# A feed-forward pass over two row groups at a time: one unit of gate or up weights for both groups of a half

## The chip, the cores and the metric

The kernel runs on one core of a Trainium2 chip. The metric is the time of one execution on the device in microseconds. Work is spread over five engines, each with its own in-order queue of instructions: TensorE (PE in the profile, with PEld for its weight loads) multiplies matrices into PSUM banks, VectorE (DVE) and ScalarE (ACT) move results out of PSUM and do elementwise work, GpSimd (POOL) does elementwise work between buffers in SBUF, and SyncE (SP) issues the transfers between SBUF and HBM.

## The reference

One layer of a hybrid encoder on 2048 rows of width 1024. The attention part (stick-breaking heads, chunked heads and a short convolution, normed per head to `y`) is the same in both kernels. What matters here is the part behind it:

```python
x = x + y @ w_out[l]                                          # output projection, 1024 x 1024
x = x + swiglu(rmsnorm(x, ffn_norm_w[l]), w_gate[l], w_up[l], w_down[l])

def swiglu(x, w_gate, w_up, w_down):                          # 1024 x 2816, 1024 x 2816, 2816 x 1024
    return (jax.nn.silu(x @ w_gate) * (x @ w_up)) @ w_down
```

The kernel holds every operand of these products as a high and a low part, and each product of a tile is three matmuls (high by high, high by low, low by high).

## The kernel before, in words

The 2048 rows are four groups of 512, numbered 0 to 3, in two halves: `HALVES` is [[3, 2], [1, 0]]. The first part of the program (`weave`, up to about 1168 us) runs the projections and the attention of both halves, then the output projection (`out_proj`) of groups 3 and 2, and makes group 3 ready for the feed-forward part (`operands`). `out_proj` writes x + y @ w_out to the HBM buffer `x1d`.

The feed-forward part is the function `ffn` (L1312). Its width of 2816 is cut into 22 tiles of 128 and `NP` = 11 pairs `p` of them. A *unit* (g, p, i) is the gate (i = 0) or up (i = 1) product of group g with pair p. It is done as seven products instead of eight (`Unit`, a1 to a5, b1, b2: Strassen's scheme in Winograd's form, two by two blocks), each of twelve matmuls of 128x256 in fp16 (`product`, L1165). The order is `units`: all 22 units of group 3, then 22 each of groups 2, 1 and 0, that is 88 units.

- **Weights of a unit.** Seven blocks, each high and low, lie in the tiles `wa` (4 blocks, 1 MB) and `wb` (3 blocks, 0.75 MB), two buffers each. For group 3 they are *made*: `unit_load` fetches two raw tiles, `unit_norm` sums squares on ScalarE (L959), `unit_scale` turns this into a power of two by a small matmul (L967) and five tiny VectorE operations, `unit_make` scales the raw tiles on ScalarE (L988), forms sums and differences on VectorE (L997, tiles `S`), casts the high parts on ScalarE (L992) and subtracts the low parts on GpSimd (L993), and stores the result to HBM (`u`). Groups 2, 1 and 0 fetch it from there (`unit_fetch`, L1017). A unit's weights are made or fetched in the turn two units ahead of it.
- **Down product.** When both units of a pair are done, `b2` splits silu(gate) * up into `gh` and `gl` (L1245, L1246, two buffers each), and `down` multiplies them by the two tiles of `w_down` (`load_down`: raw tile `wr`, then `wh` on ScalarE and `wl` on VectorE, L310, L312) and adds to the rows `x1` (L1271). It is called for half of the group's rows (24 matmuls of 128x512) in each of the next two units, so `w_down` is loaded and split once for each group and pair, 44 times two tiles. The raw tiles of gate, up and `w_down` share one ring `wr` of four buffers.
- **Side work** is put between the products of a unit by generators, a few steps at a time (`run_side`): in group 3 the per-head norms of the second half's y (`y_side`, L837 to L844, eight row tiles) and then the operands of group 2; in groups 2 and 1 the output projection of the next group (`proj_side`, one PSUM bank `av`) and then its operands. Whatever is left is run ahead of the next group (`run_all`). `operands` fetches x1, norms it (L367 to L372), turns it by 32 transposes (L908), forms seven blocks (L920) and splits them (L915, L916).

The order on TensorE is the order of the program text (`manual_schedule`). The other queues, SP's among them, are ordered when the program is built, by a planner that walks through the program with costs of its own: it takes the earliest instruction of the text whose inputs and buffers are free, so a transfer can be issued well before its place in the text, and the order it finds is fixed from then on.

Of the kernel before, what the change touches and what calls it, by code (L numbers as in the profile page):

```python
# [40 lines left out]
def trunk(ctx: ExitStack, tc: tile.TileContext, x, anw, w_in, qnw, knw, biasx, conv_w, onw, w_out,  # L41
# [466 lines left out]
    def proj_N(H, groups, units, use, prep=None):  # L508

        for g in groups:  # L510
            hh, hl = H.get(g, (None, None))
            for t in range(0, 4, 2):
                if prep is not None:
                    yield from prep.need(g, t)
                    hh, hl = H[g]
                o, bk = acc() if stream.paced else bank("av", 1)
                steps = chain.from_iterable(
                    mm3(o[:, s * 256:(s + 1) * 256], lambda k, cs=cs: hh[:, k, cs],
                        lambda k, cs=cs: hl[:, k, cs], lambda k: units[k // 4][0][:, k % 4],
                        lambda k: units[k // 4][1][:, k % 4], KT, 0.33)  # L520
                    for s, cs in ((s, slice((t + s) * 128, (t + s + 1) * 128)) for s in range(2)))
                yield from prep.beside(steps) if prep is not None else steps
                behind(bk.read(lambda g=g, t=t, o=o: use(g, t, o)))
# [354 lines left out]
    def operands(g, tmp, turn):  # L878
# [18 lines left out]
        for t in range(2):  # L897
# [20 lines left out]
            def less(a, b):  # L918
                f = tmp()
                nc.vector.tensor_tensor(f, a, b, ALU.subtract)  # L920
                return f
# [6 lines left out]
            t1 = less(b12, b11)  # L928
# [4 lines left out]
            t3 = less(b22, b12)  # L933
            parts(4, t3)
            t2 = less(b22, t1)
# [4 lines left out]
            parts(5, less(b21, t2))  # L940
# [41 lines left out]
    def unit_make(p, i):  # L982
# [12 lines left out]
        def made(op, a, b):  # L995
            f = fp.tile([128, 512], F32, name="S", tag="S", bufs=4)
            nc.vector.tensor_tensor(f, a, b, op)  # L997
            return f
# [9 lines left out]
        parts(wb[:, 2], made(ALU.subtract, a12, s2))  # L1008
# [73 lines left out]
    stream = Weights(HALF * 2 + OUT * NG)  # L1082
# [79 lines left out]
    order = [g for groups in HALVES for g in groups]  # L1162
    units = [(g, p, i) for g in order for p in range(NP) for i in range(2)]
# [16 lines left out]
    class Unit:  # L1180
# [7 lines left out]
        def got(self, f, t, c):  # L1188
            g, p, i = self.key
            ds = UD[p, i][1]  # L1190
            if i == 0:
                if (g, p) not in SG:
# [13 lines left out]
        def a1(self):  # L1206
            o = self.mul(0, acc)
            self.s1 = q("s1", 2)
            nc.scalar.copy(self.s1, o)
# [18 lines left out]

        def c_of(self, o, u, f, t):
            c = q("c", 2)  # L1230
            nc.vector.tensor_tensor(c, o, u, ALU.add)  # L1231
            self.got(f, t, c)
# [19 lines left out]
    def x1_load(g):  # L1252
        X1[g] = []
        for t in range(4):
            x1 = fp.tile([128, D], F32, name="x1", tag="x1", bufs=4)
            nc.sync.dma_start(x1, x1d[g * 4 + t])
            X1[g].append(x1)

    def down(g, p, ts):
        for t in ts:  # L1260
            cs = slice(t * 128, (t + 1) * 128)
            for c in range(2):
# [3 lines left out]
                for j, ((gh, gl), (wh, wl)) in enumerate(zip(G[g, p], DW[g, p])):  # L1266
# [6 lines left out]
    def s_tile():  # L1273
        return fp.tile([128, 512], F32, name="S", tag="S", bufs=4)

    def y_side():

        gain = gain_row("o")
        for g in HALVES[1]:
            for t in range(4):  # L1280
# [4 lines left out]
                y_norm(T, yt, gain, lambda: fp.tile([128, 512], F32, name="ysq", tag="S", bufs=4))  # L1285
                yield

    def proj_side(g):
        H = {}
        yield from out_proj(H, [g], stream, y_rows(H, [g]))  # L1290

    def operands_side(g):
        yield from operands(g, s_tile, tpb)

    second = HALVES[1]
    sides = {}
    for n, g in enumerate(order):
        steps = []
        if n == 0:
            steps.append(y_side())  # L1300
        if n + 1 < len(order):
            nxt = order[n + 1]
            if nxt in second:
                steps.append(proj_side(nxt))
            steps.append(operands_side(nxt))
        sides[g] = chain.from_iterable(steps)

    def run_side(g, n):
        for _ in islice(sides[g], n):
            pass  # L1310

    def ffn():  # L1312
        run = {}
        norms = {}
        made = {}
        made[units[0]] = unit_make(0, 0)
        made[units[1]] = unit_make(0, 1)
        for n in (2, 3):
            if n < len(units):
                unit_load(*units[n][1:])  # L1320
        x1_load(order[0])
        last = None
        n1 = 2 * NP
        for n, u in enumerate(units):
            g, p, i = u
            new = n < n1 - 2
            if new and units[n + 2] not in norms:
                norms[n + 2] = unit_norm(*units[n + 2][1:])
            if g not in BS:
                run_all(sides[units[n - 1][0]])  # L1330
            U = Unit(g, p, i, made.pop(u))
# [5 lines left out]
            per = 3 if n >= n1 else 2  # L1337
            run_side(g, per)
            U.a3()
            run_side(g, per)  # L1340
            U.a4()
            if new:
                unit_scale(*units[n + 2][1:], norms.pop(n + 2))
            if n + 2 < len(units):
                nu = units[n + 2]
                made[nu] = unit_make(*nu[1:]) if new else unit_fetch(*nu[1:])
            prev = (g, p - 1) if p else (order[order.index(g) - 1], NP - 1)
            if prev in G:
                down(*prev, (0, 1) if i == 0 else (2, 3))
            if i == 1:  # L1350
                if prev in G:
                    del G[prev], DW[prev]
                    if p == 0:
                        for t in range(4):
                            T = prev[0] * 4 + t
                            nc.sync.dma_start(out[T * 128:(T + 1) * 128, :], X1[prev[0]][t])
                        x1_load(g)
                DW[g, p] = [load_down(f) for f in (2 * p, 2 * p + 1)]
            if n + 4 < n1:
                unit_load(*units[n + 4][1:])  # L1360
            U.a5()
            run_side(g, per)
# [3 lines left out]
        g = order[-1]  # L1366
        down(g, NP - 1, range(4))
        for t in range(4):
            T = g * 4 + t
            nc.sync.dma_start(out[T * 128:(T + 1) * 128, :], X1[g][t])  # L1370

    with tc.manual_schedule(engines={mybir.EngineType.PE}):
        ffn()
# [33 lines left out]
```

## Time and profile before

| | us |
|---|---|
| median of 3 runs (range) | 2829.3 (2827.76 to 2829.47) |
| the profiled execution's own time | 2829.39 |
| its span, first to last instruction | 2827.6 |
| TensorE busy in the span | 2491.9 (88%) |
| VectorE, ScalarE, GpSimd busy | 1886.5, 1249.7, 591.3 |

The span is what the trace covers; 1.8 us of the execution lie outside it. Busy time of TensorE counts matmuls from issue to their modelled end, so it is an upper bound on useful work. The granted clock is the share of full speed that TensorE was given.

### The profile page before, as it was taken

The page shows a single profiled execution, that of the slowest core. Times are in us where ns is not written, and L with a number is a line of the kernel's source. Part 1 is how long each engine was busy: PE and PEld are TensorE (multiplying, and loading weights), DVE is VectorE, ACT ScalarE, POOL GpSimd, SP SyncE. Part 2 cuts the span into 40 slices and gives each one's busy share as a digit, 9 for nine tenths or more (in the row PEclk, how much of TensorE's full clock was granted, in tenths as well). Part 3 has the DMA queues.
Part 4 walks back from the last instruction along what each step waited for, and adds up shares of the span by engine and source line. Part 5 has one row for each costly group of instructions (what it writes and reads, how often), then busy time and mean ns, then how long its engine had stood idle before and what let it go on. Part 6 is the DMA issues. An engine that isn't in the chain of part 4 may idle for free. (4 is left out here: it accounts for less than half of the span.)

```text
span 2827.6 us, 50313 instructions
## 1 busy us (share of the span) xinstructions
PE 2491.9 (88%) x19448; PEld 2017.8 (71%) x19448; DVE 1886.5 (67%) x4181; ACT 1249.7 (44%) x2380; POOL 591.3 (21%) x635
## 2 busy tenths in 40 slices
PE   6998888997899888665878799997999997999999
PEld 4477767566776776544666688876788886888887
DVE  6478767699989868697766665444654446555555
ACT  5566656664566867655545431112321113221121
POOL 2234331103321223454644410000200002000000
PEclk9999999998899999877898899999999998999999
DMA  7443344523311565665544555454455444465442
GB/s 237 129 134 110 108 144 127 159 65 130 109 62 55 173 180 163 202 226 171 186 153 160 171 198 188 163 164 160 164 196 173 157 154 134 144 223 167 161 164 79
DMA packets 264688, 434.33 MB, mean 154 GB/s; under 512 B 79616, under 2 KB 196352, under 8 KB 253184
## 3 DMA queue, kind: packets, MB, share of 16 engines
q1 hardware_dynamic: 264448, 431.12, 47.2%
q8 instruction: 152, 2.49, 0.4%
q14 instruction: 88, 0.72, 0.1%
HBM read 321.46 MB, written 109.58 MB: 152 GB/s over the span
## 5 line engine op out<-in xcount | busy, mean ns | idle before, releaser
L1271 DVE TENSOR_TENSOR x<-tp,x 128x512 f32<-128x512 f32 x352 | 242.5, 690 | 212.7 <-PE tp L1269 212.5
L1267 PE MATMUL tp<-wh,gh 128*128 128x512 f32 x704 | 296.4, 421 | 61.7 <-ACT wh L310 24.2
L378 PE MATMUL acc<-w,hh 128*128 128x256 f16 x1152 | 325.1, 282 | 3.8 <-ACT w L273 3.8
L379 PE MATMUL acc<-w,hh 128*128 128x256 f16 x1152 | 324.7, 282 | 1.8 <-POOL w L274 1.8
L380 PE MATMUL acc<-w,hl 128*128 128x256 f16 x1152 | 324.2, 281 | 0.0
L1268 PE MATMUL tp<-wl,gh 128*128 128x512 f32 x704 | 286.8, 407 | 13.6 <-DVE wl L312 13.5
L1269 PE MATMUL tp<-wh,gl 128*128 128x512 f32 x704 | 285.0, 405 | 1.1 <-DVE gl L1246 1.1
L1196 ACT ACTIVATE sg<-c,ud 128x256 f32<-128x256 f32 x176 | 89.3, 508 | 424.3 <-DVE c L1231 406.9
L668 DVE SCALAR_TENSOR_TENSOR wtl<-tp,wth 128x512 f16<-128x512 f32 (+3 forms) x384 | 198.7, 533 | 51.5 <-ACT wth L663 50.6
L1231 DVE TENSOR_TENSOR c<-sc,u 128x256 f32<-128x256 f32 x264 | 111.1, 422 | 182.6 <-PE sc L1172 181.7
L733 DVE TENSOR_TENSOR_SCAN re<-re,zero 128x512 f32<-128x512 f32 (+3 forms) x160 | 191.4, 1196 | 39.8 <-ACT re L730 39.4
L310 ACT CAST wh<-wr 128x1024 fp32r<-128x1024 f32 x88 | 88.7, 1043 | 289.5 <-PE tp L1268 243.0
L663 ACT ACTIVATE wth<-tp 128x512 f16<-128x512 f32 (+3 forms) x384 | 173.5, 477 | 83.4 <-PE tp L659 82.1
L1267 PEld LDWEIGHTS tp<-wh,gh 128*128 128x128 f32 x704 | 138.4, 197 | 97.9 <-ACT wh L310 27.1
L1171 PE MATMUL sc<-bx,wb 128*128 128x256 f16 x704 | 192.3, 273 | 0.0
L1170 PE MATMUL sc<-bx,wb 128*128 128x256 f16 x704 | 192.3, 273 | 0.0
L1172 PE MATMUL sc<-bx,wb 128*128 128x256 f16 x704 | 192.3, 273 | 0.0
L379 PEld LDWEIGHTS <-hh 128*128 128x128 f16 x1408 | 141.7, 101 | 46.9 <-issue 20.4
L1171 PEld LDWEIGHTS <-wa 128*128 128x128 f16 x1408 | 140.0, 99 | 44.1 <-issue 26.0
L1268 PEld LDWEIGHTS tp<-wl,gh 128*128 128x128 f32 x704 | 138.6, 197 | 44.2 <-DVE wl L312 18.1
L916 POOL TENSOR_TENSOR hh<-S,hh 128x512 f16<-128x512 f32 x12 | 15.6, 1302 | 712.7 <-ACT hh L915 712.7
L1269 PEld LDWEIGHTS tp<-wh,gl 128*128 128x128 f32 x704 | 138.5, 197 | 35.9 <-DVE gl L1246 5.0
(246 smaller groups left out, 7121.6 us busy)
## 6 DMA issues: line engine op xcount, KB each, us to landing
wa<-u SPq DMA_DIRECT2D x66, 1024.0 KB, 4.9
wb<-u SPq DMA_DIRECT2D x66, 768.0 KB, 4.4
wr<-in_w_down SPq DMA_DIRECT2D x88, 512.0 KB, 4.1
w<-wd SPq DMA_DIRECT2D x48, 512.0 KB, 4.2
u<-wa SPq DMA_DIRECT2D x22, 1024.0 KB, 4.7
u<-wb SPq DMA_DIRECT2D x22, 768.0 KB, 4.4
wd<-w SPq DMA_DIRECT2D x32, 512.0 KB, 3.0
q<-qd SPq DMA_DIRECT2D x192, 64.0 KB, 2.3
```

What stands on the lines that cost most here:

```text
L378: nc.tensor.matmul(o, sh(k), mh(k), start=(k == 0), stop=False)
L379: nc.tensor.matmul(o, sh(k), ml(k), start=False, stop=False)
L380: nc.tensor.matmul(o, sl(k), mh(k), start=False, stop=(k == n - 1))
L668: nc.vector.scalar_tensor_tensor(wl[:, s], tp[:, :(b1 - b0) * 128], WSC, wh[:, s], op0=ALU.mult, op1=ALU.subtract)
L733: nc.vector.tensor_tensor_scan(re, re, zero.to_broadcast([128, N]), 1.0 if b == T else e[:, 0:1], ALU.mult, ALU.add)
L1170: nc.tensor.matmul(o, ah, bh, start=k == 0, stop=False)
L1171: nc.tensor.matmul(o, ah, bl, start=False, stop=False)
L1172: nc.tensor.matmul(o, al, bh, start=False, stop=k == 3)
L1267: nc.tensor.matmul(o, gh[:, cs], wh[:, cc], start=j == 0, stop=False)
L1268: nc.tensor.matmul(o, gh[:, cs], wl[:, cc], start=False, stop=False)
L1269: nc.tensor.matmul(o, gl[:, cs], wh[:, cc], start=False, stop=j == 1)
L1271: nc.vector.tensor_tensor(x1, o, x1, ALU.add)
```

## The change

The feed-forward part runs once per half, and the two groups of the half take turns with the same weights: after the first pair, (first, p, 0), (other, p, 0), (first, p, 1), (other, p, 1). In the first pair both units of the first group come before those of the other, while the other's operands are made. So gate and up weights are made in the first half (22 units) and fetched once in the second (22 units instead of 66 fetches), and `w_down` is loaded once per half and pair (22 times two tiles instead of 44). A unit's weights are made or fetched in the first group's turn with the unit before it; the turns a and b of one unit are the same instructions as before. `down` comes behind b2 and ahead of a2, and works off a list, one entry of two row tiles per turn. The rows `x1` of both groups are held (those of odd groups in the four tiles `w16`). The output projection of groups 1 and 0, and the operands of group 1, run between the two passes (`between`), with two PSUM banks (`acc`) instead of one.

To make room, `sg` has four buffers and `S`, `s1` and `c` have one less each; sums are written in place; three of seven splits in `operands` go from GpSimd to VectorE.

```diff
@@ proj_N
-                o, bk = acc() if stream.paced else bank("av", 1)
+                o, bk = acc()
@@ operands
-                nc.gpsimd.tensor_tensor(B[o][:, 1, :, cs], fv, B[o][:, 0, :, cs], ALU.subtract)
+                (nc.vector if o % 2 else nc.gpsimd).tensor_tensor(B[o][:, 1, :, cs], fv, B[o][:, 0, :, cs],
+                                                                  ALU.subtract)
...
-            t1 = less(b12, b11)
+            t1 = less(b12, b11, b11)
...
@@ class Unit, c_of
-                SG[g, p] = [fp.tile([128, 512], F32, name="sg", tag="sg", bufs=2) for _ in range(2)]
+                SG[g, p] = [fp.tile([128, 512], F32, name="sg", tag="sg", bufs=4) for _ in range(2)]
...
-                nc.scalar.activation(sg, c, AF.Silu, scale=ds)
+                nc.vector.tensor_tensor(sg, o, u, ALU.add)
+                nc.scalar.activation(sg, sg, AF.Silu, scale=ds)
...
@@ x1_load
+            if g % 2 == 0:
+                x1 = fp.tile([128, D], F32, name="x1", tag="x1", bufs=4)
+            else:
+                x1 = f32(wp.tile([128, 2, D], F16, name="w16", tag="w16").rearrange("p j c -> p (j c)"))
...
@@ ffn
+    def ffn(half, sides, tail):
+        first, other = HALVES[half]
+        weights = [(p, i) for p in range(NP) for i in range(2)]
+        turns = [(g, 0, i) for g in (first, other) for i in range(2)]
+        turns += [(g, p, i) for p in range(1, NP) for i in range(2) for g in (first, other)]
+        new = half == 0
...
+        begin(0)
+        DW[0] = [load_down(f) for f in (0, 1)]
+        begin(1)
+        for w in range(2, 4 if new else 0):
+            unit_load(*weights[w])
+        for g in HALVES[half]:
+            x1_load(g)
...
+            if g == other and p == 0 and i == 0:
+                run_all(sides)
+            U = Unit(g, p, i, made[p, i])
             U.a1()
             if last is not None:
                 last.b1()
                 last.b2()
+                lg, lp, li = last.key
+                if li == 1:
+                    due += [(lg, lp, (0, 1)), (lg, lp, (2, 3))]
+            if todo is not None:
+                tg, tp, ts = todo
+                down(tg, tp, ts)
+                if ts[0] == 2:
+                    del G[tg, tp]
+                    if tg == other:
+                        del DW[tp]
+                        if tp + 1 < NP:
+                            DW[tp + 1] = [load_down(f) for f in (2 * tp + 2, 2 * tp + 3)]
+            if (g == first and p > 0) or (g == other and (p, i) == (0, 1)):
+                if w + 1 in norms:
+                    unit_scale(*weights[w + 1], norms.pop(w + 1))
+                begin(w + 1)
+            if new and g == other:
+                if 4 <= w + 3 < len(weights):
+                    unit_load(*weights[w + 3])
+                if w + 2 < len(weights):
+                    norms[w + 2] = unit_norm(*weights[w + 2])
             U.a2()
+            side(3)
             U.a3()
+            side(3)
             U.a4()
+            side(3)
             U.a5()
...
+        for tg, tp, ts in due:
+            down(tg, tp, ts)
+            if (tg, ts[0]) == (first, 2):
+                store(first)
+            if tg == other:
+                for _ in islice(tail, 4):
+                    pass
+        store(other)
+        run_all(rest)
+        run_all(tail)
+
+    def between():
...
+        yield from out_proj(H, [a], W, rows)
+        yield from beside_of(out_proj(H, [b], W, rows), operands(a, s_tile, tpb))
...
+        ffn(0, (operands(HALVES[0][1], s_tile, tpb), y_side()), between())
+        ffn(1, (operands(HALVES[1][1], s_tile, tpb), iter(())), iter(()))
```

`begin(n)` makes (first half) or fetches (second half) the weights of unit n once; `side(n)` runs n steps of the other group's operands in the first group's first two turns, and of `y_side` after them.

## Rows read from the trace of the kernel before

**Rows 1.** Busy time by engine (page): us, share of the span, instructions.

```profile
PE 2491.9 (88%) x19448; PEld 2017.8 (71%) x19448; DVE 1886.5 (67%) x4181; ACT 1249.7 (44%) x2380; POOL 591.3 (21%) x635
```

**Rows 2.** Windows: length, busy PE, PEld, DVE, ACT, POOL, clock, DMA, GB/s.

```profile
1171.50:1669.80 498.30, 361.61 (x2376) 290.94 (x2377) 351.58 (x668) 260.09 (x430) 248.77 (x176) 0.85 0.55 185
1669.80:2078.50 408.70, 380.02 (x2827) 324.06 (x2826) 213.30 (x386) 86.38 (x148) 19.70 (x14) 0.97 0.51 170
2078.50:2482.20 403.70, 378.56 (x2826) 323.78 (x2824) 212.18 (x385) 86.51 (x148) 18.81 (x14) 0.98 0.47 159
2482.20:2827.60 345.40, 338.93 (x2450) 288.85 (x2448) 191.12 (x349) 66.17 (x112) 0.00 (x0) 1.00 0.47 158
1373.40:1637.80 264.40, 217.77 (x1432) 176.86 (x1430) 171.79 (x311) 141.08 (x231) 122.62 (x91) 0.90 0.51 166
2500.00:2800.00 300.00, 300.00 (x2213) 256.96 (x2211) 165.98 (x306) 60.13 (x102) 0.00 (x0) 1.00 0.48 161
```

**Rows 3.** Timeline of PE, first matmuls of units: start us, us, instruction.

```profile
1892.71 0.27 PE L1170 MATMUL acc<-hh,wa 128*128 128x256 f16 x1
1910.34 0.27 PE L1170 MATMUL acc<-hh,wa 128*128 128x256 f16 x1
...
2702.53 0.27 PE L1170 MATMUL acc<-hh,wa 128*128 128x256 f16 x1
2702.64 0.27 PE L1171 MATMUL acc<-hh,wa 128*128 128x256 f16 x1
...
2717.22 0.27 PE L1170 MATMUL acc<-hh,wa 128*128 128x256 f16 x1
```

**Rows 4.** Waits of PE, 1373 to 1638 us: total us, times, longest.

```profile
PE tp L1267 <- ACT wh L310: 17.8, 6, 3.3
PE sc L1170 <- DVE u L1227: 12.7, 5, 3.3
PE tp L1267 <- ACT gh L1245: 11.0, 6, 2.9
PE tp L1268 <- DVE wl L312: 4.1, 6, 1.8
PE tp L1269 <- DVE gl L1246: 1.1, 6, 0.2
```

**Rows 5.** Waits of all engines, 1373 to 1638 us.

```profile
DVE S L997 <- ACT wr L988: 15.4, 5, 3.8
```

**Rows 6.** Groups of VectorE in 1373 to 1638 us: busy us, mean ns, idle before.

```profile
L997 DVE TENSOR_TENSOR S<-wr 128x512 f32<-128x512 f32 x28 | 29.3, 1045 | 15.5 <-ACT wr L988 15.4
```

**Rows 7.** Timeline of PE, a group's change: start us, us, instruction, idle before it.

```profile
1945.59 0.27 PE L1170 MATMUL acc<-hh,wa 128*128 128x256 f16 x1
...
1966.09 0.48 PE L908 MATMUL tp<-ident,xf 128*128 128x128 f32 x1 [13.46 <-DVE xf L372]
...
2005.03 0.27 PE L1170 MATMUL acc<-hh,wa 128*128 128x256 f16 x1
```

**Rows 8.** Groups in 1945 to 2010 us: the transposes of one `operands`.

```profile
L908 PE MATMUL tp<-ident,xf 128*128 128x128 f32 x32 | 5.7, 318 | 15.5 <-DVE xf L372 13.5 <-ACT S L910 2.0
```

**Rows 9.** Timeline of PE, the first units of group 3.

```profile
1171.46 0.28 PE L1170 MATMUL acc<-hh,wa 128*128 128x256 f16 x1 [3.93 <-DMA x<-x1d]
...
1199.47 0.16 PE L967 MATMUL av<-ws,ones 128*128 128x1 bf16 x1 [12.71 <-ACT junk L959]
```

**Rows 10.** Groups of VectorE in 1171 to 1330 us: head norms, first and last of ten.

```profile
L842 DVE TENSOR_TENSOR yt<-yt,yry 128x1024 f32<-128x1024 f32 x8 | 10.7, 1337 | 0.1
...
L147 DVE TENSOR_SCALAR yry<-yry 128x16 int32<-128x16 int32 x8 | 1.3, 166 | 0.1
```

**Rows 11.** Timeline of PE, the end of the span.

```profile
2810.39 0.50 PE L1267 MATMUL tp<-wh,gh 128*128 128x512 f32 x1 [2.27 <-ACT gh L1245]
...
2823.01 0.39 PE L1269 MATMUL tp<-wh,gl 128*128 128x512 f32 x1
```

**Rows 12.** DMA issues (page): KB each, us from issue to landing.

```profile
wa<-u SPq DMA_DIRECT2D x66, 1024.0 KB, 4.9
```

More of the change, by code (lines that the diff above doesn't have):

```diff
@@ L939, in operands @@
             parts(3, b21)
-            parts(5, less(b21, t2))
+            parts(5, less(b21, t2, b21))
         BS[g] = B
@@ L993, in parts, with made @@
             nc.gpsimd.tensor_tensor(dst[:, 1, :], f, dst[:, 0, :], ALU.subtract)
-        def made(op, a, b):
-            f = fp.tile([128, 512], F32, name="S", tag="S", bufs=4)
+        def made(op, a, b, f=None):
+            f = s_tile() if f is None else f
             nc.vector.tensor_tensor(f, a, b, op)
@@ L1007, in unit_make @@
         parts(wb[:, 1], a22)
-        parts(wb[:, 2], made(ALU.subtract, a12, s2))
+        parts(wb[:, 2], made(ALU.subtract, a12, s2, s2))
         UW[p, i] = wd["u", p, i] = [dp.tile([128, n, 2, 512], F16, name=f"u{p}_{i}{n}") for n in (4, 3)]
@@ L1207, in a1 @@
             o = self.mul(0, acc)
-            self.s1 = q("s1", 2)
+            self.s1 = q("s1", 1)
             nc.scalar.copy(self.s1, o)
@@ L1273, in s_tile @@
     def s_tile():
-        return fp.tile([128, 512], F32, name="S", tag="S", bufs=4)
+        return fp.tile([128, 512], F32, name="S", tag="S", bufs=3)
     def y_side():
@@ L1284, in y_side @@
                 yield
-                y_norm(T, yt, gain, lambda: fp.tile([128, 512], F32, name="ysq", tag="S", bufs=4))
+                y_norm(T, yt, gain, lambda: fp.tile([128, 512], F32, name="ysq", tag="S", bufs=3))
                 yield
[L1288 to L1313, printed above, removed]
-        norms = {}
[L1315 to L1321, printed above, removed]
+    def store(g):
+        for t in range(4):
+            T = g * 4 + t
+            nc.sync.dma_start(out[T * 128:(T + 1) * 128, :], X1[g][t])
@@ new lines, in ffn, with side, begin @@
+    def ffn(half, sides, tail):
[4 more added lines that the diff above has]
+        new = half == 0
+        made = {}
+        norms = {}
+        started = set()
+        sides, rest = sides
+        def side(n):
+            for _ in islice(sides if g == first and p == 0 else rest, n):
+                pass
+        def begin(n):
+            if n in started or n >= len(weights):
+                return
+            started.add(n)
+            made[weights[n]] = unit_make(*weights[n]) if new else unit_fetch(*weights[n])
+        begin(0)
[5 more added lines that the diff above has]
+            x1_load(g)
@@ L1322, in ffn @@
         last = None
-        n1 = 2 * NP
-        for n, u in enumerate(units):
+        due = []
+        split = 0
+        for n, u in enumerate(turns):
             g, p, i = u
[L1326 to L1331, printed above, removed]
+            w = weights.index((p, i))
+            todo = due.pop(0) if due else None
+            if g == other and p == 0 and i == 0:
+                run_all(sides)
+            U = Unit(g, p, i, made[p, i])
@@ L1365, in ffn @@
         last.b2()
[L1366 to L1370, printed above, removed]
+        due += [(*last.key[:2], (0, 1)), (*last.key[:2], (2, 3))]
+        for tg, tp, ts in due:
[4 more added lines that the diff above has]
+                for _ in islice(tail, 4):
+                    pass
+        store(other)
+        run_all(rest)
+        run_all(tail)
+    def between():
+        W = stream2
+        H = {}
+        a, b = HALVES[1]
+        rows = y_rows(H, HALVES[1])
+        yield from out_proj(H, [a], W, rows)
+        yield from beside_of(out_proj(H, [b], W, rows), operands(a, s_tile, tpb))
+    stream2 = Weights(OUT * 2)
+    stream2.paced = False
     with tc.manual_schedule(engines={mybir.EngineType.PE}):
-        ffn()
+        ffn(0, (operands(HALVES[0][1], s_tile, tpb), y_side()), between())
+        ffn(1, (operands(HALVES[1][1], s_tile, tpb), iter(())), iter(()))
 def kernel(**inputs):
```

52 lines of the change are left out of this document (11 added, 41 removed).

## Prediction

> **What bounds the kernel now.** I read the page's busy times first: TensorE is busy for 88% of the span, VectorE for 67%, nothing else comes near [rows 1]. That is a mean over stages, so the windows came next, one for each of the four groups of the feed-forward part. Here the reader is to see that the same 22 units take 498.3 us for group 3, 408.7 and 403.7 us for groups 2 and 1, and 345.4 us for group 0; that from 2500 to 2800 us TensorE is busy all the time at a granted clock of 1.00 (2.4 GHz), with weights fetched for every unit; and that group 3, where the weights are made, has a mean clock of 0.85 (part of it at the 1.2 GHz level) and GpSimd at half [rows 2]. Third, the timeline of PE gives the price of an unhindered unit: two starts of group 0 lie 14.69 us apart, and two starts with a share of the output projection between them 17.63 us, so that share costs 2.94 us [rows 3].
>
> From these comes the floor of the stretch from 1171.5 to 2827.6 us (1656.1 us). 88 units at 14.69 are 1292.7 us. The second half's output projection went over 16 units for each of two groups, 2 x 16 x 2.94 = 94.1. The transposes of three operand sets are 3 x 5.7 = 17.1 [rows 8]. From the last matmul to the end are 4.6 us [rows 11]. Sum 1408.5: the kernel loses 247.6 us there. By a rule of the Trainium skill (Perfetto Trace Analysis, Identifying the Most-Contended Engine) one judges headroom by the busy time of weight loads rather than of matmuls. PEld is busy for 1227.6 us in the four windows, and 0.857 of the time where TensorE never waits [rows 2], which makes 1433 us of work and 223 lost; by matmul time it would be 197. Weight loads take longer at the lower clock, so I go by the count of units.
>
> Where is it lost? In 1373 to 1638 us, 264.4 us hold 13 units, whose floor is 191.0: 73.4 lost, 5.65 a unit. The waits of PE name 46.7 of them: 34.0 for the down product's operands (w_down's parts 17.8 and 4.1, gh and gl 11.0 and 1.1) and 12.7 for `u` on VectorE [rows 4]. The other 26.7 go with a clock of 0.90 [rows 2]. The wait for `u` has its cause on VectorE's own queue: it stood 15.4 us for ScalarE to scale the raw tiles, then did the sums S at 1045 ns each, with the evictions behind them [rows 5, 6]. Group 3's opening is worse: a wait of 12.71 us for the norm of the third unit's raw tiles [rows 9]. And at a group's change the operands come late: 59.4 us from one start to the second after it, 13.46 of them in one wait for a normed row tile [rows 7].
>
> **The change part by part.** The time up to 1171.5 us stays, but for six splits of group 3's operands that go to VectorE amid the attention: at the 1045 ns of a like subtraction [rows 6] at most 6 us, if VectorE were the bound there; if GpSimd was, a gain as large. I take 0.
>
> *Halved fetches.* 66 fetches of `wa` become 22 [rows 12], those of `wb` likewise, and 88 tiles of `w_down` become 44. In 2500 to 2800 us all of that ran beside a TensorE that never waited, so its loss is worth 0. ScalarE and VectorE have 44 splits less each, in turns where they had room.
>
> *Making, spread over two turns.* This is the gain. Before, one unit was made in each unit's time; now one in two, and in the first half there are 44 turns to hide 22. Down's operands have a turn more: gh is made in the turn ahead of the one in which `down` uses it, and w_down's raw tiles find their ring freed by a making that ended early in the turn, some 9 us ahead of use (a2 to a5, a1, b1 and b2 lie between, 84 matmuls that start every 0.11 us [rows 3], 9.2 us). So I let the 34.0 us and their share of the low clock go: 34.0 + 26.7 x 34.0/46.7 = 53.4 over 13 units, 4.1 a unit. What is late next is `u`: VectorE still waits in its queue for the scaled raw tiles. Per making it cost (12.7 + 26.7 x 12.7/46.7)/13 = 1.5 us, and 20 makings (two precede the pass) keep that: 31 us. Bounds: 0, where a2 to a5 and the next a1 cover the block, and 5.65 x 20 = 113, where all of the old loss stays; I stay at the row for the same wait. Behind the scaling wait on ScalarE stand the copy s1 and the silu, and for these only VectorE and the unit after wait.
>
> *The first pass's opening.* The wait for the third unit's norm goes, as that unit is not scaled before the fourth turn. In its place TensorE waits for the other group's operands, whose transposes now stand in the first two turns. The nearest row is a group's change: 59.4 - 2 x 14.69 - 5.7 = 24.4 us [rows 7, 8]. The first products still wait for the first making: 4 us, like the wait that stands ahead of them now (bounds 0 and the 12.71 that followed) [rows 9]. Then the eight tiles of head norms fall into three turns instead of four units: ten groups on VectorE, the first 10.7 and the last 1.3 us, 55.6 in all [rows 10]. Three turns are 9.2 + 14.7 + 14.7 = 38.6 us on TensorE, in which VectorE owes 0.55 x 38.6 = 21 us of its own [rows 2] and 5 for a making. That is 82 against 39, 43 too much; I take 25, since some of it can be done in the wait for the operands (bounds 0 and 43). Sum 53.
>
> The moved splits enter here. Before, all seven were on GpSimd; now VectorE has three of them in each of two passes over the rows. The sums S ran at 1045 ns in the mean beside GpSimd [rows 6]. The Trainium skill says (SBUF — State Buffer, Who interferes with whom) that a VectorE instruction with two SBUF inputs and a GpSimd instruction that reads SBUF block each other for the whole instruction. The mean of 1045 ns fits that without showing it. By that rule work split over both is partly one queue, and the sum would lose the 6 x 1.05 = 6 us of an `operands` that the split could save. The sum counts 0 for the split either way.
>
> *Between the passes.* All of 94.1 us is in the floor, and now stands bare: no unit lies between its matmuls, so its 16 results ask for an eviction every 5.9 us (94.1/16), which two banks allow. The bare wait for gh is 2.27 us, and the 48 matmuls behind it take 12.6 us where 24 take 5.5 (14.69 - 9.2), as at the end of the span [rows 11]: 4. I add 3 for the first turned rows and 6 for the operands of group 1, which run beside the second group's projection (bounds 0 and the 24.4 of a bare change). 13.
>
> *The second pass's opening.* Group 0's operands need rows that the projection has only just stored, and eight transfers of x1 may go ahead of them in SP's queue. 24.4 by the row; I take 26 (bounds 20 and 45, the latter with four transfers of 4.9 us [rows 12] ahead). After it this pass is group 0 of today, without waits. Its end keeps the 4 us around gh; `down` owes four entries there instead of two, but turns earlier had none, and the floor counts each once.
>
> Losses: 53 + 31 + 13 + 26 + 4 = 127. 1171.5 + 1408.5 + 127 = 2707.0 us of span, and with the 1.8 us outside it 2708.8. The profiled execution's 2829.4 is the median of the runs (2829.3), so I predict 2709 us, 4.3% less.
>
> **The rivals.** *Making stays bare* (0.15): VectorE's queue is fixed when the program is built, and if the planner puts the sums S ahead of evictions each time, 5.65 us stay at each of 20 makings: 2709 + 113 - 31 = 2791. For: the 15.4 us wait [rows 5]. Against: 34.0 of 46.7 us belonged to down's operands.
>
> *Cover all through* (0.08): a2 to a1 cover the sums, and the head norms find room in the waits: 2709 - 31 - 25 = 2653.
>
> *The raw ring* (0.04): gate, up and w_down share four raw tiles, and now w_down's pair must pass between units loaded two turns ahead. If a unit's norm is late at each scaling, TensorE's queue stops as at 1199 us, 12.7 us for each of 20 makings [rows 9]: 2709 + 254 - 31 = 2932. It decides the sign from (2829 - 2709 + 31)/20 = 7.6 us a making. Against: raw tiles are asked for two turns (29 us) ahead of their norm.
>
> *It doesn't do what it says* (0.03): the halved fetches are worth nothing by themselves, and if the turns bring as much new waiting as they take, the time stays at 2829.
>
> **How the numbers follow.** Forecast 0.70, with a range of its own of 2670 to 2755 (makings 0 to 2.5 us, norms 0 to 43, openings at either bound). The range for 8 in 10 goes to 2645, to hold full cover, and to 2785, short of the bare making's centre; about 0.18 is left out. Faster by over 0.2% (5.7 us, about what a measurement of this kernel can tell from no change): the first three cases, 0.93. Same 0.02 and slower 0.05 share the last two.
>
> **What would show it.** Right: windows of pairs of turns in the first pass near 29.4 to 33 us with PE's waits only for `u`; in the second pass 14.69 between starts throughout; two openings with waits of 20 to 30 us on `xf`; VectorE full for some 60 us behind the first. Wrong: waits for wh, wl or gh inside the passes, waits of L967 on L959, or a projection between the passes well over 107 us.

## The result, and the profile after

The kernel with the change takes 2760.0 us (median of 4 runs, 2757.7 to 2761.0), the kernel before on the same chip 2828.5 us (4 runs, 2826.9 to 2829.5). The ratio is 0.9757, with a 95% interval of 0.974 to 0.9774: 68.5 us or 2.4% faster. 2709 us were forecast, 120 us faster; the direction was right and the time lies in the range for 8 in 10 (2645 to 2785), but above the forecast's own, 2670 to 2755, and two fifths of the gain are missing.

The page's busy times first. They hardly differ from [rows 1]: TensorE is at 89% where it was at 88%, VectorE again at 67%.

```profile
PE 2460.5 (89%) x19448; PEld 2002.0 (73%) x19448; DVE 1852.3 (67%) x4161; ACT 1203.8 (44%) x2336; POOL 555.5 (20%) x611
```

Cut by stage, they say more (columns as in [rows 2]; the first column is the stretch, the second its length). A turn is one unit in its place in the new order; a pass, the feed-forward part of one half, has 44. The stretches are: the first pass's first eight turns in two parts, its next 35 turns, from the start of its last turn to the second pass, and the second pass.

```profile
1167.48:1240.42 72.94, 35.69 (x260) 28.70 (x261) 45.30 (x81) 39.29 (x69) 29.11 (x22) 0.71 0.57 186
1240.42:1356.63 116.21, 78.40 (x525) 64.36 (x523) 89.57 (x217) 40.03 (x69) 47.04 (x29) 0.84 0.44 149
1356.63:1926.43 569.80, 533.71 (x3816) 449.32 (x3814) 368.23 (x661) 215.65 (x374) 159.63 (x119) 0.97 0.33 107
1926.43:2073.98 147.55, 137.61 (x1095) 119.12 (x1093) 70.19 (x122) 33.40 (x55) 10.90 (x8) 0.98 0.61 203
2073.98:2756.00 682.02, 653.68 (x4786) 558.55 (x4783) 356.62 (x681) 123.07 (x226) 10.60 (x8) 0.98 0.23 81
```

I set each stretch against its floor, from the prices of the prediction: a product 1.31 us (14.69 - 5.51 = 9.18 for seven), a share of `down` 5.5, the transposes of one `operands` 5.7, a second output projection 94.1, the end 4.6. The first turn has only five products (b1 and b2 come a turn later), and the first four shares of `down` fall into turns 4 to 7.

| stretch | length | floor | lost | forecast |
|---|---|---|---|---|
| turns 1 to 3 of the first pass (1167.48 to 1240.42) | 72.9 | 19 x 1.31 + 5.7 = 30.6 | 42.3 | 28.4 |
| turns 4 to 8 | 116.2 | 35 x 1.31 + 4 x 5.5 = 67.9 | 48.3 | 25 + 3 x 1.55 = 29.6 |
| turns 9 to 43 | 569.8 | 35 x 14.69 = 514.2 | 55.6 | 17 x 1.55 = 26.4 |
| last turn and projection | 147.55 | 14.69 + 2.6 + 22 + 94.1 + 5.7 = 139.1 | 8.4 | 13 |
| second pass to the end | 682.0 | 308 x 1.311 + 44 x 5.51 + 5.7 + 4.6 = 656.6 | 25.4 | 26 + 4 |
| sum | | 1408.5 | 180.0 | 127 |

So 53 us more are lost than forecast. The pass begins 4.0 us earlier (1167.48 against 1171.5), which leaves the 49 us between the spans of 2756.0 and 2707.0 us.

The second pass is as it was read. From its fourth turn on, two starts with a share of `down` between them lie 14.66 to 14.69 us apart, as in [rows 3], and behind its opening TensorE has no wait over 0.3 us. PE's waits from 2074 us on (the others are 0.2 us each):

```profile
PE tp L908 <- DVE xf L372: 17.0, 1, 17.0
PE sc L1168 <- DVE u L1227: 5.3, 2, 2.8
```

The 35 turns of the first pass show what the forecast missed. The waits for `wh`, `wl` and `gh` of [rows 4] are gone, as forecast; but so is the wait for `u` of L1227, on which the forecast had put what was left. All of PE's waits from 1357 to 1926 us are these:

```profile
PE tp L1265 <- DVE x L1269: 29.0, 8, 3.6
PE tp L1265 <- DVE w L1269: 7.1, 9, 0.8
```

They come in pairs, one of 3.6 us and one of 0.8 us for every two makings. `down` finds no free PSUM bank, because VectorE has not yet added an earlier result to x1. The cause is on VectorE's queue (timeline of DVE in a turn that makes a unit; start, length, instruction, idle time before it):

```profile
1400.13 0.69 DVE L997 TENSOR_TENSOR S<-wr 128x512 f32<-128x512 f32 x1 [0.34 <-ACT wr L988]
1400.91 1.48 DVE L997 TENSOR_TENSOR S<-S,wr 128x512 f32<-128x512 f32 x1
1402.31 1.64 DVE L997 TENSOR_TENSOR S<-wr 128x512 f32<-128x512 f32 x1
1403.88 0.41 DVE L1197 TENSOR_TENSOR c<-acc,s 128x256 f32<-128x256 f32 x1
1404.32 0.93 DVE L1198 SCALAR_TENSOR_TENSOR sg<-sg,ud,c 128x256 f32<-128x256 f32 x1
1406.31 1.64 DVE L997 TENSOR_TENSOR S<-wr,S 128x512 f32<-128x512 f32 x1 [1.05 <-POOL wa L993]
1407.87 0.41 DVE L1197 TENSOR_TENSOR c<-sc,u 128x256 f32<-128x256 f32 x1
...
1411.51 1.28 DVE L1269 TENSOR_TENSOR x<-tp,x 128x512 f32<-128x512 f32 x2
```

The fourth sum is a12 - s2, and the change writes it over s2 (`made(ALU.subtract, a12, s2, s2)`). It must wait until GpSimd has read s2 for its split. Behind it stand seven operations on the unit's results and then the x1 adds, in a fixed order, and TensorE's queue stops (timeline of PE, the same turn):

```profile
1408.23 0.39 PE L1267 MATMUL tp<-wh,gl 128*128 128x512 f32 x1
1412.25 0.79 PE L1265 MATMUL tp<-wh,gh 128*128 128x512 f32 x1 [3.63 <-DVE x L1269]
1412.84 0.63 PE L1266 MATMUL tp<-wl,gh 128*128 128x512 f32 x1
1413.27 0.63 PE L1267 MATMUL tp<-wh,gl 128*128 128x512 f32 x1
```

Behind the wait the same matmuls start every 0.43 us where they started every 0.23 before it, about half the speed, that of the 1.2 GHz level, until 1415 us. Over the whole kernel, the idle time ahead of the sums and their lengths (min/median/max) read in the kernel before:

```profile
L997 DVE TENSOR_TENSOR S<-wr,S x22: 677/1164/1646, 1174.7 to 1638.5; 128x512 f32<-128x512 f32 x22
...
  ACT wr L988: 20.0, 7
  POOL wa L993: 1.9, 2
```

and in the kernel after:

```profile
L997 DVE TENSOR_TENSOR S<-wr,S x22: 1623/1641/1643, 1173.0 to 1900.4; 128x512 f32<-128x512 f32 x22
...
  POOL wa L993: 31.0, 22
  ACT wr L988: 8.0, 20
```

Two waits for GpSimd in the whole kernel have become one at every making. The wait alone does not set the loss: every second making it is 1.50 us (that of 1440.78), with three operations between the sum and the x1 adds instead of seven, and TensorE then stands for 0.79 us and not 3.63. The other loss is in the opening (timeline of PE; the transfers of `xf` are shown further below):

```profile
1207.25 3.16 PE L908 MATMUL tp<-ident,xf 128*128 128x128 f32 x12 [30.02 <-DVE xf L372]
1254.86 0.80 PE L1265 MATMUL tp<-wh,gh 128*128 128x512 f32 x1 [7.59 <-DVE w L1269]
1288.32 0.80 PE L1265 MATMUL tp<-wh,gh 128*128 128x512 f32 x1 [16.92 <-DVE w L1269]
```

The first wait is for the other group's operands, the later ones for evictions behind the head norms: VectorE is busy for 39.1 of the 44 us from 1246 to 1290. By some 9.7 us of that, operations of the norms and of the unit are lengthened beside GpSimd's multiplication by the gain (L843, see the last section).

### The profile page after: what moved, and what is told of

Same layout as the page of the kernel before. It is cut to its first block, busy times and chain, and to the rows that moved or that the text cites. A ratio compares the mean times of both kernels' runs of the same rounds, so it can differ in the third digit from the quotient of the medians.

```text
span 2756.0 us, 50003 instructions
## 1 busy us (share of the span) xinstructions
PE 2460.5 (89%) x19448; PEld 2002.0 (73%) x19448; DVE 1852.3 (67%) x4161; ACT 1203.8 (44%) x2336; POOL 555.5 (20%) x611
## 4 chain that ended last, share of the span: by engine, by line
PE 40%; DVE 6%; POOL 4%; issue 2%; DMA 2%; ACT 2%; SPq 1%; ACTq 0%; DVEq 0%; POOLq 0%
PE tp L1265 6%; PE tp L1266 5%; PE tp L1267 5%; PE sc L1168 5%; PE sc L1170 5%; PE sc L1169 5%; POOL wa L993 3%; PE acc L1169 2%; PE acc L1170 2%; PE acc L1168 2%; DMA x1d<-xs 1%; POOL wb L993 1%; ACT wr L988 1%; DVE S L997 1%; DVE sg L1198 1%
## 5 line engine op out<-in xcount | busy, mean ns | idle before, releaser
L378 PE MATMUL acc<-w,hh 128*128 128x256 f16 x1408 | 392.5, 279 | 3.8 <-ACT w L273 3.8
L379 PE MATMUL acc<-w,hh 128*128 128x256 f16 x1408 | 392.3, 279 | 1.8 <-POOL w L274 1.8
L380 PE MATMUL acc<-w,hl 128*128 128x256 f16 x1408 | 392.1, 278 | 0.0
L1194 ACT ACTIVATE sg<-sg,ud 128x256 f32<-128x256 f32 x176 | 86.9, 505 | 256.6 <-DVE sg L1193 255.3
L1269 DVE TENSOR_TENSOR x<-tp,x 128x512 f32<-128x512 f32 x176 | 120.6, 689 | 112.9 <-PE tp L1267 106.5
L1269 DVE TENSOR_TENSOR w<-tp,w 128x512 f32<-128x512 f32 x176 | 120.4, 688 | 91.9 <-PE tp L1267 84.9
L1168 PEld LDWEIGHTS <-wa 128*128 128x128 f16 x1408 | 138.9, 99 | 39.9 <-issue 17.0
L379 PEld LDWEIGHTS <-hh 128*128 128x128 f16 x1408 | 140.7, 100 | 31.8 <-issue 5.3
L1169 PEld LDWEIGHTS <-wa 128*128 128x128 f16 x1408 | 139.3, 99 | 24.5 <-issue 8.1
L378 PEld LDWEIGHTS <-hh 128*128 128x128 f16 x1408 | 141.0, 100 | 21.3 <-issue 2.0
```

The costliest lines, as they stand in the source:

```text
L378: nc.tensor.matmul(o, sh(k), mh(k), start=(k == 0), stop=False)
L379: nc.tensor.matmul(o, sh(k), ml(k), start=False, stop=False)
L380: nc.tensor.matmul(o, sl(k), mh(k), start=False, stop=(k == n - 1))
L1168: nc.tensor.matmul(o, ah, bh, start=k == 0, stop=False)
L1169: nc.tensor.matmul(o, ah, bl, start=False, stop=False)
L1269: nc.vector.tensor_tensor(x1, o, x1, ALU.add)
```

## The experiments

The theory at first was that VectorE is short of time all through the first pass. The rivals were: that only the placing of the head norms is wrong; that the halved fetches, worth 0 in the forecast, carry the gain; and that one order or one buffer, not VectorE's load, holds each stage. Ratios are to the kernel before on the same chip; that of the change is 0.9757.

**Head norms, one step a turn**, over the whole first pass.

```diff
+        def norm_step():
+            if not (g == first and p == 0):
+                next(rest, None)
...
             U.a2()
-            side(3)
+            if g == first and p == 0:
+                side(3)
...
+            norm_step()
             U.a5()
```

(The edit of `side(3)` is the same behind a2, a3 and a4.)

> The changed kernel with the head norms of the second half's y spread: one step of them in each turn of the first pass from the third on, instead of nine a turn in three turns. Theory: VectorE, overfilled by them in the turns 1240 to 1343 us, is what makes TensorE wait there (four turns take 102.5 us where 58.8 would do), and elsewhere it has room; so some 30 us go, 2730 us. Rival 1: VectorE is short all through the first pass, the norms cost the same spread out: 2755 to 2765. Rival 2: those turns are long by the first makings (three in them) and not by the norms: at most 10 us go, 2750.

2758.6 us, ratio 0.9747 (0.9718 to 0.9777): nothing gained, as the first rival had it. Windows of this kernel, for turns 4 to 8 and for the next 35:

```profile
1240.87:1327.09 86.22, 74.70 (x524) 62.09 (x522) 57.14 (x112) 36.78 (x62) 30.71 (x22) 0.92 0.33 112
1327.09:1924.74 597.65, 543.18 (x3817) 455.62 (x3815) 402.83 (x769) 224.24 (x386) 176.96 (x126) 0.95 0.35 115
```

The opening gives back 30.0 us, and the turns after it lose 27.9. They have no room for a norm as they stand.

**The sums on GpSimd** (`nc.gpsimd` for `nc.vector` in `made`; there are four of them).

> The changed kernel with the four sums of each making on GpSimd instead of VectorE. Theory: in the first pass's steady turns VectorE's queue, held by the sums at 0.7 to 1.6 us each, is late with the evictions of the down product (waits of 3.63 and 0.78 us plus the low clock behind them: 65.1 us for four turns where 58.8 would do); so the 6.3 us of each four turns go, some 50 us over the pass, 2705 to 2715 us. Rival: GpSimd then has eleven operations of 1.2 to 1.6 us in a row for a making, the weights are late and TensorE waits for them: no gain or a loss, 2755 to 2800.

2768.3 us, ratio 0.9787 (0.9761 to 0.9812): no gain, by the medians 8 us slower than the change, with intervals that overlap. With the sums gone from VectorE, every fourth turn or so still takes 21 us. So load alone isn't it: something else had come late. VectorE's queue, and the transfers of SP ahead of it, in one such turn:

```profile
1500.59 1.23 DVE L312 TENSOR_TENSOR wl<-wr,wh 128x1024 fp32r<-128x1024 f32 x1 [5.09 <-ACT wh L310]
```

```profile
1492.31 0.33 SPq L1011 DMA_DIRECT2D u<-wb  x1
1492.68 0.44 SPq L308 DMA_DIRECT2D wr<-in_w_down  x1
```

The second raw tile of w_down is asked for behind the store of the made weights, which waits for GpSimd's longer making.

**Fetches doubled again** in the second pass: each turn fetches the unit's weights, as before the change, and x44 of `wa` stand where the change has x22.

```diff
-            U = Unit(g, p, i, made[p, i])
+            U = Unit(g, p, i, made[p, i] if new else fetched.pop(n))
...
+            if not new and 2 <= n + 1 < len(turns):
+                fetched[n + 1] = unit_fetch(*turns[n + 1][1:])
```

> The changed kernel, but in the second pass each turn fetches its unit's weights anew, one turn ahead, so both groups of the half fetch them: 44 fetches there instead of 22, as often for each turn as the kernel before. Theory: the fetches were hidden before and are hidden now, their halving is worth nothing: 2758 to 2763 us, starts of turns still 14.66 to 14.69 us apart. Rival: with w_down and x1 beside them, or with buffers free only a turn ahead, they wait: 2 us or more a turn, 2800 and up.

2760.9 us, ratio 0.9757 (0.9731 to 0.9784). The second pass's halved fetches of `wa` and `wb` are worth nothing, as forecast. The halved loads of w_down stay in this kernel; no run tests them by themselves.

**The operands' fetches ahead.** Their first step is run before the first making, and the other group's x1 is fetched after its operands.

```diff
+        next(sides)
         begin(0)
...
-        for g in HALVES[half]:
-            x1_load(g)
+        x1_load(first)
...
                 run_all(sides)
+                x1_load(other)
```

> The changed kernel with the first two row tiles of the other group's operands fetched ahead of the first making in the program text, and that group's x1 loaded two turns later. Theory: the wait of 30.0 us for normed row tiles in the first pass's opening is SyncE's queue, where these transfers stood behind the stores of both makings and the raw tiles of two more (issued at 1195.9 us, their data ready some 25 us earlier); ahead of them, 15 to 22 us of that wait go, and a few of the 17.0 us in the second pass: 2735 to 2745 us. Rival: the norm is late for ScalarE and VectorE, which are in the makings until 1186 us, or the norms behind just wait longer: 2755 us.

2747.2 us, ratio 0.9713 (0.9688 to 0.9738): 12 to 13 us, a little short of what was expected. About half of it comes from each opening: the first turn behind the first pass's opening starts 6.5 us earlier (1350.15), the fifth turn of the second pass 12.2 us earlier (2131.35 against 2143.57). The fourth tile was still asked for behind the weight loads, at 1194.21 us, and a second wait of 12.40 us stayed.

**Two attempts on the makings**: the sums on GpSimd and besides w_down's raw tiles asked for four turns ahead, ahead of the store; and the early raw tiles alone. The request that both share:

```diff
...
                     unit_load(*weights[w + 3])
+                    if i == 1:
+                        for f in (2 * p + 2, 2 * p + 3):
+                            if f < 2 * NP:
+                                down_raw[f] = fetch_down(f)
```

> The five sums of a making on GpSimd, as in the run with the sums on GpSimd, and besides the two raw tiles of w_down asked for four turns before they are split, ahead of the u<-wb store. Theory: with the sums gone from VectorE, what was left of the loss is the second raw tile of w_down, whose transfer stands on SP's queue behind the store of a making that ends late (request at 1492.68 behind the store at 1492.31, VectorE at wl L312 for 5.09 us). Then every turn of the first pass from the ninth on takes 14.6 to 14.8 us, and the 6.3 us lost in every fourth turn go: nine of them, 57 us, so 2768.3 becomes 2710 to 2730. Rival: GpSimd's own making, longer by five sums, is the limit; the wait then moves to wa or to the x1 adds and the time stays at 2755 or above.

> Only the early request of the w_down raw tiles, with the sums left on VectorE. Theory: in the kernel with the change the fourth turn is held by the sums that stand on VectorE ahead of the x1 adds, and no raw tile is late there, so nothing moves: 2755 to 2765, every fourth turn still 19.9 to 21.4 us. Rival: the raw tiles of w_down are late in that kernel too and the sums only stand behind them; then 20 us or more go, 2740 or below.

2778.4 us, ratio 0.9834 (0.9821 to 0.9848), for both, and 2755.7 us, 0.9756 (0.9741 to 0.9771), for the raw tiles alone. The second is as expected. The first refutes my reading of the run with the sums on GpSimd: the late raw tile was not all. ScalarE now stands 3.48 and 3.69 us for GpSimd's sums (until 1417.09 and 1421.68), and its order puts the squares of the next unit's norm, which wait for a transfer, ahead of the casts to `gh`, and VectorE stands for them (timelines of ACT and of DVE):

```profile
1425.98 1.06 ACT L964 ACTIVATE junk<-wr 128x1024 bf16<-128x1024 f32 x1 [1.71 <-DMA wr<-in_w_up]
1426.94 0.19 ACT L964 ACTIVATION_READ_ACCUMULATOR junk<-wr 128x1 bf16 x1
1427.03 0.60 ACT L1245 CAST gh<-sg 128x512 fp32r<-128x512 f32 x1
```

```profile
1427.67 0.69 DVE L1246 TENSOR_TENSOR gl<-sg,gh 128x512 fp32r<-128x512 f32 x1 [7.92 <-ACT gh L1245]
```

From 1360 to 1930 us VectorE stands 92.9 us for `gh`, in 18 waits, where it stood 15.0 us in 13 in the kernel with the change. Each time all four sums leave VectorE, the making ends later and holds another queue.

**All of that together**, with the four tiles of the operands fetched at once (`fetch(1)` behind `fetch(0)`).

> All that was found so far together: sums on GpSimd, w_down's raw tiles early, the head norms in steps of one per turn over the first pass, and the fetches of the operands' four tiles ahead of the x1 loads and weight loads at both openings. Theory: the three losses are separate once VectorE has room: some 50 us of makings, some 20 of the head norms in the opening and 15 to 25 of the operand fetches go, 2670 to 2700. Rival: the head norms, spread out, fall beside makings again and cost there what they save in the opening, as in the run with the norms spread alone: 2700 to 2725.

2768.8 us, ratio 0.9796 (0.9783 to 0.981). Slower than theory and rival alike: the waits for `gh` stay (54.3 us in 12, from 1340 to 1920 us), and the makings lose more than the openings bring.

**The splits back on GpSimd.**

```diff
-                (nc.vector if o % 2 else nc.gpsimd).tensor_tensor(B[o]...
+                nc.gpsimd.tensor_tensor(B[o]...
```

> Only the splits of the operands of odd number put back from VectorE to GpSimd. Theory: they lie beside waits for fetched tiles in both openings and are worth nothing: 2756 to 2764. Rival: VectorE is the engine that is full in the first opening, and the twelve splits there, off it, give back 5 to 10 us: 2750 to 2755.

2755.3 us, ratio 0.9754 (0.9741 to 0.9767): the time lies between the two that were expected, but the ratio is that of the change, so the split of that work is worth nothing that can be told from no change, as forecast.

**Only the fourth sum on GpSimd**, where the split that it must follow stands anyway.

```diff
-        parts(wb[:, 2], made(ALU.subtract, a12, s2, s2))
+        nc.gpsimd.tensor_tensor(s2, a12, s2, ALU.subtract)
+        parts(wb[:, 2], s2)
```

> Only the last of the four sums of a making, a12 - s2, which overwrites s2, put on GpSimd, where the split of s2 that it must follow stands too; the other three sums stay on VectorE. Theory: what costs the fourth turn is that VectorE, at this sum, stands still until GpSimd has split s2 (1.05 us at 1406.31) and then runs the sum beside GpSimd (1.64 us), with the evictions of the unit and the x1 adds behind it in a fixed order; these 2.7 us are most of the 3.63 us that TensorE waits, and with them goes the low clock behind it. Then four turns take 60 to 62 us where they took 65.1, nine times: 27 to 45 us less, 2715 to 2735. Rival: any work that leaves VectorE comes back as a later wait on ScalarE's or GpSimd's order, as with all four sums; 2750 or more.

2735.7 us, ratio 0.9665 (0.965 to 0.968): 26 us less than the change, just under the 27 to 45 expected. PE's waits from 1357 to 1900 us, and eight turns in one window:

```profile
PE sc L1169 <- DVE u L1215: 16.2, 8, 2.7
PE tp L1266 <- DVE x L1270: 10.6, 8, 1.3
```

```profile
1369.58:1494.21 124.63, 118.33 (x874) 100.56 (x872) 79.47 (x149) 50.89 (x88) 41.79 (x33) 1.00 0.34 110
```

The waits of 3.63 us are now 1.33, the clock is 1.00 where it was 0.97, and four turns take 62.3 us where they took 65.1. The 35 turns take 549.1 us (1351.65 to 1900.73) where they took 569.8: 20.7 of the 26 us; some 5 more come in the turns before them, which hold three makings. Of the 20.7 us only 6.3 are waits of TensorE (29.8 are left of 36.1 over these turns); the rest goes with the clock, as the half-speed stretch behind each 3.63 us is gone. The wait for `u` of L1215 is new: VectorE stands 33.3 us in 8 waits for ScalarE to cast w_down's second raw tile, which is asked for behind the store of the made weights again:

```profile
1479.22 1.23 DVE L312 TENSOR_TENSOR wl<-wr,wh 128x1024 fp32r<-128x1024 f32 x1 [3.97 <-ACT wh L310]
```

The kernel with the change has no such wait. The early raw tiles beside this one moved sum were not tried. How much of the gain is the wait of 1.05 us, which the change's edit in place brought, and how much the sum's own 1.64, this run does not part. A fourth buffer `S` in place of the edit was not tried.

**Adding up.** That sum, the four fetches ahead at both openings, and the head norms in the other group's turns, which hold no making; and the same with the head norms left in the first turns.

> The last sum on GpSimd, the fetches of the operands' four tiles ahead of the x1 loads and weight loads at both openings, and the head norms over the turns of the other group from the second pair on, which hold no making. Theory: the gains add up, some 35 us of makings, 13 to 20 of the fetches and 20 to 30 of the head norms, less 1 to 2 us for each of eight turns with a norm: 2680 to 2705. Rival: a turn with a norm costs the 5 us that it cost with one norm step a turn; then 2705 to 2730.

> The last sum on GpSimd and the fetches of the operands' four tiles ahead of the x1 loads and weight loads at both openings, with the head norms where the change has them, in the first turns. Theory: the two gains are in different stretches and add up: the last sum alone gave 2735.7, and the fetches 10 to 18 us more, so 2716 to 2727; and spreading the head norms costs in later turns as much as it saves in the opening, so that this is no slower than 2729.2, the time with the norms spread as well. Rival: in the opening VectorE, full of head norms, is the limit whatever is fetched when; the earlier operands only bring a longer wait behind the norms, and the time stays within 4 us of 2735.7, while the norms spread were what brought 2729.

2729.2 us, ratio 0.9644 (0.9631 to 0.9657), and 2720.0 us, ratio 0.9618 (0.9604 to 0.9633). The last sum and the fetches add up; the norms, spread, cost 7 us (by the ratios) to 9 us more than they save, though their turns hold no making, as the rival had it. The second is the fastest version found: 108 us faster than the kernel before, and by the ratios 39 faster than the change. Its first transposes' waits, beside the 30.02 us above:

```profile
1193.59 1.12 PE L910 MATMUL tp<-ident,xf 128*128 128x128 f32 x4 [16.54 <-DVE xf L372]
1206.69 1.09 PE L910 MATMUL tp<-ident,xf 128*128 128x128 f32 x4 [5.87 <-DVE xf L372]
```

What became shorter stood on SP's queue. In the kernel with the change, three of the four transfers are issued behind stores and weight loads:

```profile
1160.30 0.32 SPq L893 DMA_DIRECT2D xf<-x1d  x1
1177.17 2.41 SPq L308 DMA_DIRECT2D wr<-in_w_down  x2
1186.76 2.66 SPq L952 DMA_DIRECT2D wr<-in_w_gate  x2
1189.52 4.52 SPq L952 DMA_DIRECT2D wr<-in_w_up  x2
1195.87 1.37 SPq L893 DMA_DIRECT2D xf<-x1d  x3
```

and here all stand ahead of them:

```profile
1162.99 0.32 SPq L893 DMA_DIRECT2D xf<-x1d  x1
1170.82 1.27 SPq L893 DMA_DIRECT2D xf<-x1d  x3
```

**One bank for the projection between the passes**, as it was when the projection ran beside the units.

```diff
-                o, bk = acc()
+                o, bk = acc() if stream.paced else bank("av", 1)
```

> Only the second output projection, between the passes, put back on the one bank it had before the change, where it used to run beside the FFN. Theory: its 16 groups of products then wait for their eviction with nothing beside them, 0.4 to 1.2 us each, and the stretch between the passes grows by 7 to 20 us: 2767 to 2780. Rival: the transposes and operands beside it fill that; nothing moves.

2767.6 us, ratio 0.9778 (0.9762 to 0.9793), as expected. The stretch grows from 147.55 to 156.34 us, with waits of PE that the change does not have there:

```profile
PE av L378 <- DVE xs L869: 14.4, 15, 2.5
```

## Why the prediction was right, and where its size was off

**Right in direction.** The old loss of 5.65 us a unit was, by its larger part, the wait for down's operands, and that is gone: none of those waits over 0.2 us is left in the passes. Whether one making for two units did it, or the turn more that `down` leaves for its operands, the prediction did not part, and no run does. The halved fetches (0), the moved splits (0) and the second pass's 14.69 us a turn held. The projection between the passes lost 8.4 us where 13 were forecast, and the second opening and the end 25.4 where it was 30.

**The step that failed: the makings**, 31 us forecast, 65 found: 55.6 / 17 = 3.3 us each, measured in the 35 turns and above the 2.5 that the forecast's own range allowed, and by an estimate at that price 10 for the three in the opening. The prediction took the price of the old wait for `u`, "1.5 us", and its cause, ScalarE's scaling. That wait is gone. In its place stands one that the change made: the fourth sum, written over s2, waits for GpSimd at each of 22 makings (31.0 us of VectorE, against 1.9 before), runs at 1.64 us beside GpSimd, and the x1 adds behind it hold `down`. So the sign "PE's waits only for `u`" did not come true. The diff shows the edit and the prediction gave it no term. Moving that one sum took back 26 us; which part of them the wait is, stays open. The rival "making stays bare" was nearer in mechanism (sums ahead of evictions) and too dear in price: 3.3 us, not 5.65.

**The operands in the first opening**, 28.4 forecast, 42.3 measured. "24.4" came from a change of groups where three of the transfers were issued 5 us behind the last stores of their rows (1957.16 after 1952.20); here it was 32 us (1195.87 after 1164.20), with stores and weight loads between them on SP's queue. For the second pass the prediction had seen that queue; for the first it had not asked. With the fetches ahead, in the fastest version, the three turns take 62.3 us instead of 72.9.

**The head norms**, 25 forecast, within bounds of 0 and 43: 48.3 less 10 for three makings leaves 38.5, an estimate; with the norms spread these turns gave back 30.0. The wait for the operands covered none of them: the first two row tiles `yt` were asked for at 1210.44 us, behind that wait, though VectorE stood idle for 14.81 us up to 1203.34. By the estimate the excess of 43 us that the prediction worked out from rows was nearer than the 25 taken from it.

These three are 34, 14 and 13.5 us too small; the other terms and the earlier start give back 13, by chance. That is the 49 us between forecast and measured span.

What is left open: the fastest version still loses 40 us in the first pass's 35 turns (554.4 against a floor of 514.2) and 42 us in turns 4 to 8, where the head norms stand (110.4 against 67.9), and its transposes still wait 22.4 us for `xf`.

## What to carry to other kernels

When a change saves a buffer by writing a result over its input, look for who else reads that input: the new wait stands in the queue of the engine that writes, and what it costs depends on what stands behind it there. Work taken off the busiest engine helps only as far as it doesn't lengthen a chain that another in-order queue waits for; here one sum of four moved gained 26 us, and all four moved gained nothing. For each transfer that a stage begins with, read what stands ahead of it on its queue; here that, and not its own length, set when it landed.

## What the hardware showed that was not expected

The sum that begins ahead of GpSimd's first split (1400.13 us) takes 0.69 us, at 21 of 22 makings, and those beside its splits 1.46 to 1.64: the medians over the kernel of the three lines of sums went from 0.69, 0.94 and 1.16 us to 1.29, 1.48 and 1.64. Evictions with one input in PSUM stayed at 0.41 to 0.43 us beside the same splits, while L1198, with its operands in SBUF, went from 0.48 to 0.93. This fits the rule weighed in the prediction (the Trainium skill, SBUF — State Buffer, Who interferes with whom), by which a VectorE instruction with two inputs in SBUF contends with a GpSimd instruction that reads SBUF. The rows bear out that spreading such work over both engines is partly one queue.

The sums are lengthened by up to 0.95 us, beside splits of 1.2 to 1.6 us. The head norms show that it can be the whole of GpSimd's instruction (timelines of POOL and of DVE, kernel with the change):

```profile
1247.18 2.34 POOL L843 TENSOR_TENSOR yt<-yt,gain 128x1024 f32<-128x1024 f32 x1 [16.11 <-DVE yrt L154]
```

```profile
1247.37 2.18 DVE L158 SCALAR_TENSOR_TENSOR yrt<-yrt,yry 128x16 f32<-128x16 f32 x1
```

The operation on 16 columns takes 0.16 to 0.18 us where none stands beside it; here it begins behind GpSimd's and ends with it, to 0.03 us. Six of the eight multiplications by the gain hold one operation of VectorE so, by 1.5 to 2.1 us, some 11.7 us together in turns 4 to 8. Putting that multiplication elsewhere was not tried.
